# First phase of a hybrid decoder layer: column-group order of two small matmul blocks, GpSimd's elementwise work on other engines, and new places of the side steps

## Chip, cores and metric

The kernel runs on one core of one Trainium2 chip. The metric is the device time of one execution in microseconds (us). Engines are named as in the profile: PE (TensorE), PEld (its weight loads), DVE (VectorE), ACT (ScalarE), POOL (GpSimd), SP (SyncE, which here only issues DMAs).

## What is computed

One layer for 512 tokens of width 1024. The part that the change touches is the first phase: an input projection, two recurrent mixers (HGRN2 and S5) and two gates. In the reference, cut to this part:

```python
h = _rmsnorm(x, norm_mix_g)
q_raw, f_raw, i_raw, og_raw, u_raw, gate_hg, gate_s5 = jnp.split(h @ w_in, SPLITS, axis=-1)
# HGRN2, 4 heads of 128, chunks of 64 tokens
f = lb + (1.0 - lb) * sigmoid(f_raw); k = 1.0 - f; q = silu(q_raw)
b = cumsum(log(f)) within a chunk
scores = (q * exp(b - b_ref)) @ (k * exp(b_ref - b)).T, lower triangle
o = scores @ v + (q * exp(b)) @ S_prev
S  = decay * S_prev + (k * exp(b_last - b)).T @ v
y_hg = o * rsqrt(mean(o * o)) * norm_g * silu(og_raw)
# S5, 32 groups: x_t = Abar x_{t-1} + Bbar u_t,  y_t = Re(C x_t) + D u_t
g = gelu(y); y_s5 = g * sigmoid(g @ glu_w + glu_b)
merged = sigmoid(gate_hg) * (y_hg @ w_branch_hg) + sigmoid(gate_s5) * (y_s5 @ w_branch_s5)
```

Behind it come an output projection, a conv-gated MLP, a per-layer embedding and a last norm. The change does not touch them.

## The kernel before

**Big matmuls.** Every product with a weight matrix is made of three matmuls in fp32r (L231 to L233, the function `mm3`): weights and activations are split into a high and a low part, and high times high, high times low and low times high are added in PSUM. I call such a group of three a triple. Weights come in chunks through SP's DMA queue; ACT makes the high part and DVE the low part of each chunk (`split`, L243 and L244), up to three chunks ahead of their use.

**Order on PE.** PE's instructions are issued in the order in which the program is written (`manual_schedule`). For the other engines the framework's scheduler chooses the order, by its own estimate of times, at most guided by `high_priority`. The main line of the first phase is `phase_u` (32 triples for the S5 input u, then 8 for f of head 0), then the pieces in `ORDER`: projections of heads h0 to h3 (f, q, og, 8 triples each), v (32), and eight gates g0 to g7 (16 each).

**Side steps.** The mixers' small matmuls are woven into the main line by a planner. `clock` counts estimated microseconds: 0.65 for each triple, and 1.7 ns for each stationary or moving column, whichever are more, for each small matmul. After each triple, `tick` looks at the side generators (`hg_all`, `s5_side`, `r1_side`); one whose due time has come runs up to its next `yield`, and the value that it yields is the delay until its next step. The table `WAIT` holds these delays. A head of HGRN2 takes these steps: its elementwise chain (`hg_side`, L487 to L518), `psc` (scores), `pk` (transposes), `pu` (state updates), `pso` (outputs), `pms` (sum of squares). A block of S5 takes: tables Fr, Fi, Hr, Hi (`s5_tables`, L724 to L743), `ps5k` (kernel), `ps5t` (transposes), `ps5v` (inputs to states, then a scan on DVE), `ps5y` (outputs). All small matmuls are in plain fp32; each shows in the trace as two records. L172 is the helper `mm`, so they are told apart by their tiles.

**Column groups.** An output that starts at PSUM partition 0, 32, 64 or 96 and has 64 or 32 stationary columns occupies a part of PE's columns, a column group. `ps5v` (L777) already takes its two 64-column groups in turn, and `ps5k` (L747, L750) its four 32-column groups. `psc` takes for each of four token tiles five matmuls: one of 64 columns between the two chunks, two of 64, two of 32. `ps5y` takes for each of four pairs of groups Fr, two T and Fi, all with 128 stationary columns.

**Elementwise work on GpSimd.** L496, L497, L513, L573 and L574 of each head, L725, L728, L739 and L742 of each S5 block. GpSimd also issues the DMAs of u, of the S5 kernels (`d_k`, then T) and of the S5 outputs.

**Set-up of S5.** `s5_setup` (L616 to L701), some hundred small DVE instructions at high priority, issued behind `phase_u` in the program.

Of the kernel before, what the change touches and what calls it, by code (L numbers as in the profile page):

```python
# [8 lines left out]
F32 = mybir.dt.float32  # L9
F32R = mybir.dt.float32r  # L10
I32 = mybir.dt.int32
AF = mybir.ActivationFunctionType
ALU = mybir.AluOpType
# [3 lines left out]
P = 128  # L17
# [15 lines left out]


WAIT = {
    "r": [16.5, 17.5],
    "hg": [[19.5, 3.5, 4.5, 5, 7],
           [13.5, 3.5, 5.5, 5, 10],
           [18.0, 4, 4, 5.5, 7.5],
           [22.0, 3.5, 4, 9, 6.5]],  # L40
    "s5": [[20, 0, 2, 13, 0],
           [9, 2, 16.5, 12.5, 4.0],
           [7, 1.5, 5.5, 15, 0],
           [5, 4.0, 12.5, 14, 12.0]],
}

ORDER = "h0 v h1 g0 h2 g1 g2 h3 g3 g4 g5 g6 g7".split()
# [66 lines left out]
def hybrid_kernel(ctx: ExitStack, tc: tile.TileContext, a):  # L114
# [56 lines left out]
    def mm(out, w, x, start=True, stop=True, **kw):  # L171
        E.matmul(out, w, x, start=start, stop=stop, **kw)  # L172
        clock[0] += max(w.shape[-1], x.shape[-1]) * 1.7e-3
# [8 lines left out]
    def split_w(i):  # L182
        split_w_.pop(i)()

    early = {}

    def w_chunk(i, off):
        n = chunk_size(plan[i])
# [6 lines left out]
    def emit_w(dst=None):  # L195
        i = wstate["next"]
        n = chunk_size(plan[i])
        off = wstate["off"]
        wst = early.pop(i, None)
        if wst is None:  # L200
            wst = wp.tile([P, CW], F32, tag="wst", bufs=2, name=f"wst{i}")
            nc.sync.dma_start(wst[:, :n], w_chunk(i, off))
        if dst:
            whi, wlo = dst
        else:
            whi = wp.tile([P, CW], F32R, tag="whi", bufs=LOOK + 1, name=f"whi{i}")
            wlo = wp.tile([P, CW], F32R, tag="wlo", bufs=LOOK + 1, name=f"wlo{i}")

        def do():
            split(whi[:, :n], wlo[:, :n], wst[:, :n])  # L210

        if i < 3:
            split_w_[i] = do
        else:
            with tc.high_priority():
                do()
        wstate["off"] += P * n
        wstate["next"] += 1
        return whi, wlo
# [21 lines left out]
    def split(hi, lo, src):  # L241

        S.activation(hi, src, AF.Copy)  # L243
        V.tensor_tensor(out=lo, in0=src, in1=hi.bitcast(F32), op=ALU.subtract)  # L244

    def act_pair(name):
        return (ap_.tile([P, KD, T], F32R, tag="ahi", name=name + "h"),
# [237 lines left out]
    def hg_side(h):  # L485
# [3 lines left out]
        S.activation(sq, q, AF.Sigmoid)  # L489
        so_ = hgt("e1", h)  # L490
        S.activation(so_, og, AF.Sigmoid)
        V.tensor_scalar(out=f, in0=f, scalar1=olb[:, h:h + 1], scalar2=lbt[:, h:h + 1],
                        op0=ALU.mult, op1=ALU.add)
        kk = hgt("kk", h)
        V.tensor_scalar(out=kk, in0=f, scalar1=-1.0, scalar2=1.0, op0=ALU.mult, op1=ALU.add)
        G.tensor_tensor(out=q, in0=q, in1=sq, op=ALU.mult)  # L496
        G.tensor_tensor(out=og, in0=og, in1=so_, op=ALU.mult)  # L497
        S.activation(f, f, AF.Ln)
        b = hgt("b", h)
        V.tensor_tensor_scan(out=b, data0=smask, data1=f, initial=0.0, op0=ALU.mult, op1=ALU.add)  # L500
# [9 lines left out]
        kc = f  # L510
        V.tensor_tensor(out=kc, in0=f, in1=kk, op=ALU.mult)
        V.tensor_tensor(out=e2, in0=e2, in1=kk, op=ALU.mult)
        G.tensor_tensor(out=e1, in0=e1, in1=q, op=ALU.mult)  # L513
        V.tensor_tensor(out=q, in0=q, in1=b, op=ALU.mult)
        qa, ka, qb = e1, e2, q
        dec = ch(b)[:, :, CH - 1]
# [7 lines left out]
        HC = CH // 2  # L524
        for t in range(4):
            c0 = t * P
            mm(psc[0:CH, c0 + CH:c0 + P], kc[:, c0:c0 + CH], qb[:, c0 + CH:c0 + P])
            for n, x0 in ((CH, HC), (HC, 0)):
                for o in (CH, 0):
                    mm(psc[o:o + n, c0 + o + x0:c0 + o + x0 + HC], ka[:, c0 + o:c0 + o + n],  # L530
                       qa[:, c0 + o + x0:c0 + o + x0 + HC])

        V.tensor_tensor(out=pr(kc)[:, :, 0], in0=pr(kc)[:, :, 0],
                        in1=bc(pr(b)[:, :, 1, CH - 1:CH], P, 4, CH), op=ALU.mult)
# [35 lines left out]
        S.activation(osq, pso, AF.Square)  # L570
        osh = hgt("e1", h, dt=F32R)
        osl = hgt("e2", h, dt=F32R)
        G.tensor_scalar(out=osh, in0=osq, scalar1=1.0, scalar2=0.0, op0=ALU.mult, op1=ALU.add)  # L573
        G.tensor_tensor(out=osl, in0=osq, in1=osh.bitcast(F32), op=ALU.subtract)  # L574
        yield WAIT["hg"][h][4]
        pms = small_ps("pms")
        E.matmul(pms, onesr, osh, start=True, stop=False)
# [32 lines left out]
    def tmp2(*shape):  # L610
        n = math.prod(shape)
        names = "abc"[:len(shape)]
        pat = f"p ({' '.join(names)}) -> p {' '.join(names)}"
        return [t[:, :n].rearrange(pat, **dict(zip(names, shape))) for t in tv]

    def s5_setup():  # L616
# [67 lines left out]
        V.tensor_tensor(out=ni, in0=ni, in1=tq, op=ALU.subtract)  # L684
        V.tensor_tensor(out=nr, in0=nr, in1=den, op=ALU.mult)
        V.tensor_tensor(out=ni, in0=ni, in1=den, op=ALU.mult)
        t1, t2 = tmp2(GP, 16)
        cmul(V, br_, bi_, bc(nr.unsqueeze(2), P, GP, 16), bc(ni.unsqueeze(2), P, GP, 16), bcp[:, 0], bcp[:, 1],
             t1, t2)
# [24 lines left out]
    def s5_tables(b):  # L714
        gs = slice(b * 4, b * 4 + 4)
        Fr = sp.tile([P, 4, 9, 16], F32, tag="Fr", name=f"Fr{b}")
        Fi = sp.tile([P, 4, 9, 16], F32, tag="Fi", name=f"Fi{b}")
        sh = (P, 4, 9, 16)
        cr = bc(bcp[:, 2, gs].unsqueeze(2), *sh)
        ci = bc(bcp[:, 3, gs].unsqueeze(2), *sh)  # L720
        ar = bc(Ar[:, gs].unsqueeze(3), *sh)
        ai = bc(Ai[:, gs].unsqueeze(3), *sh)
        t1, t2 = tmp2(4, 9, 16)
        V.tensor_tensor(out=t1, in0=cr, in1=ar, op=ALU.mult)  # L724
        G.tensor_tensor(out=t2, in0=ci, in1=ai, op=ALU.mult)  # L725
        V.tensor_tensor(out=Fr, in0=t1, in1=t2, op=ALU.subtract)
        V.tensor_tensor(out=t1, in0=cr, in1=ai, op=ALU.mult)
        G.tensor_tensor(out=t2, in0=ci, in1=ar, op=ALU.mult)  # L728
        V.scalar_tensor_tensor(out=Fi, in0=t1, scalar=-1.0, in1=t2, op0=ALU.mult, op1=ALU.subtract)
        Hr = sp.tile([P, 4, 8, 16], F32, tag="Hr", name=f"Hr{b}")  # L730
        Hi = sp.tile([P, 4, 8, 16], F32, tag="Hi", name=f"Hi{b}")
        sh = (P, 4, 8, 16)
        ar = bc(Ar[:, gs, 1:9].unsqueeze(3), *sh)
        ai = bc(Ai[:, gs, 1:9].unsqueeze(3), *sh)
        br = bc(br_[:, gs].unsqueeze(2), *sh)
        bi = bc(bi_[:, gs].unsqueeze(2), *sh)
        t1, t2 = tmp2(4, 8, 16)
        V.tensor_tensor(out=t1, in0=ar, in1=br, op=ALU.mult)
        G.tensor_tensor(out=t2, in0=ai, in1=bi, op=ALU.mult)  # L739
        V.tensor_tensor(out=Hr, in0=t1, in1=t2, op=ALU.subtract)  # L740
        V.tensor_tensor(out=t1, in0=ar, in1=bi, op=ALU.mult)
        G.tensor_tensor(out=t2, in0=ai, in1=br, op=ALU.mult)  # L742
        V.tensor_tensor(out=Hi, in0=t1, in1=t2, op=ALU.add)  # L743
        yield WAIT["s5"][b][0]
        pk = small_ps("ps5k")
        for i in range(4):
            E.matmul(pk[i * 32:(i + 1) * 32, 0:P], Bbr[:, b * 4 + i],  # L747
                     Fr[:, i, 1:9].rearrange("p t q -> p (t q)"), start=True, stop=False)
        for i in range(4):
            E.matmul(pk[i * 32:(i + 1) * 32, 0:P], Bbi[:, b * 4 + i],  # L750
                     Fi[:, i, 1:9].rearrange("p t q -> p (t q)"), start=False, stop=True)
        clock[0] += 0.6
        kt = sp.tile([P, 8, 16], F32, tag="kt", name=f"kt{b}")
        S.activation(kt, pk[:, 0:P].rearrange("p (t q) -> p t q", t=8), AF.Copy)
        V.scalar_tensor_tensor(out=kt[:, 7], in0=e16, scalar=d16[:, b:b + 1], in1=kt[:, 7],
                               op0=ALU.mult, op1=ALU.add)
        G.dma_start(d_k[b].rearrange("p g t -> g p t")[:, :, 0:128], kt.rearrange("p t q -> p (t q)"))
        G.dma_start(bigs[b][1], dram_ap(d_k, b * 16 * 8 * 240, [[16, 8], [240, P], [1, P]]))
        yield WAIT["s5"][b][1]
        et = sp.tile([P, 2, 4, P], F32, tag="et", name=f"et{b}")  # L760
        for ri, h_ in enumerate((Hr, Hi)):
            pt = small_ps("ps5t")
            for i in range(4):
                E.transpose(pt[:, i * P:(i + 1) * P], h_[:, i].rearrange("p s q -> p (s q)"), ident)
            S.activation(et[:, ri], pt.rearrange("p (g n) -> p g n", g=4), AF.Copy)
        Fb[b] = (Fr, Fi, et)
        yield WAIT["s5"][b][2]

    def s5_states(b):
# [36 lines left out]
        yield WAIT["s5"][b][3]  # L806
        py = small_ps("ps5y")
        for i in range(4):
            gp = b * 4 + i
            o = py[:, i * P:(i + 1) * P]  # L810
            mm(o, Fr[:, i, 0:8].rearrange("p t q -> p (t q)"), st[:, 0, i].rearrange("p r c -> p (r c)"),
                     start=True, stop=False)
            for r in range(2):
                g = gp * 2 + r
                mm(o[:, r * NC5:(r + 1) * NC5], bigs[b][1][:, i * 2 + r], bigs[b][0][:, i * 2 + r], start=False, stop=False,
                         skip_group_check=True)
            mm(o, Fi[:, i, 0:8].rearrange("p t q -> p (t q)"), st[:, 1, i].rearrange("p r c -> p (r c)"),
                     start=False, stop=True)
        yl = bigs[b][2]
        S.activation(yl, py.rearrange("p (g c) -> p g c", g=8), AF.Copy)  # L820
        G.dma_start(lifted(d_y, b), yl)
# [66 lines left out]
    phase_u()  # L888
    hg_setup()
    with tc.high_priority():  # L890
        s5_setup()
    for b in range(4):
        s5_load(b)
    hg = side(hg_all())
# [310 lines left out]
```

## Time and profile before

| what | value |
|---|---|
| time, median of 3 runs | 791.29 us (791.24 to 791.9) |
| profiled execution, its own time | 792.42 us |
| its span, first to last instruction | 790.3 us |
| PE busy | 772.0 us, 98% of the span |
| DVE, ACT, POOL busy | 520.6, 358.9, 104.8 us |
| mean granted TensorE clock | 0.994 |

The first phase fills about the first 283 us of the span. In a row of groups, the columns are line, engine, operation, tiles (out<-in), shapes and count, then busy us and mean ns of one, then the engine's idle us just before them and what ended it. In the timeline the columns are start us, us, engine, line, operation; rows with a count are merged. Matmuls are pipelined, so their durations overlap, and what one costs is read from start to start.

### The profile page before, as it was taken

How to read it: one execution, taken by the hardware profiler on the slowest of the kernel's cores; microseconds unless marked ns; L12 is line 12 of the kernel's file. 1: busy time of each engine (PE TensorE's matmuls, PEld its weight loads, DVE VectorE, ACT ScalarE, POOL GpSimd, SP SyncE). 2: the span in 40 equal slices, each digit the busy share in tenths (PEclk: the TensorE clock that was granted, in tenths of full speed). 3: DMA queues.
4: the chain of work that ended last, by engine and by line, in shares of the span. 5: the costliest groups of instructions: out<-in, count | busy, mean ns of one | idle time of the engine just before them, and what ended most of it. 6: DMA issues, size and time to landing. Idle time of an engine off the chain costs nothing.

```text
span 790.3 us, 9971 instructions
## 1 busy us (share of the span) xinstructions
PE 772.0 (98%) x3806; PEld 638.4 (81%) x3806; DVE 520.6 (66%) x827; ACT 358.9 (45%) x470; POOL 104.8 (13%) x133
## 2 busy tenths in 40 slices
PE   9899999999999999999999999999999999999996
PEld 7687877888888778888888888888888888888885
DVE  7998885888583576475887667776677134243654
ACT  7345373563753942253543434434444133233565
POOL 2044351331521100032000000000000001010000
PEclk9999999999999999999999999999999999999999
DMA  9472424223343233523232232232332333224511
GB/s 339 161 186 79 131 67 111 81 70 99 102 104 107 74 107 106 193 101 107 80 107 94 93 107 84 103 108 81 107 99 88 93 94 107 69 93 140 178 53 54
DMA packets 27039, 86.10 MB, mean 109 GB/s; under 512 B 4720, under 2 KB 4864, under 8 KB 26992
## 3 DMA queue, kind: packets, MB, share of 16 engines
q1 hardware_dynamic: 22608, 77.58, 29.9%
q0 software_dynamic: 3664, 6.84, 3.9%
q10 hardware_dynamic: 720, 1.05, 0.4%
q8 instruction: 30, 0.49, 0.3%
q14 instruction: 17, 0.14, 0.1%
HBM read 80.72 MB, written 4.69 MB: 108 GB/s over the span
## 4 chain that ended last, share of the span: by engine, by line
PE 71%; DMA 2%; ACT 2%; DVE 1%; issue 1%; POOL 0%; DVEq 0%; ACTq 0%
PE pdn L233 5%; PE pdn L231 5%; PE pdn L232 5%; PE puv L231 5%; PE pug L231 5%; PE puv L233 5%; PE pug L233 5%; PE pug L232 5%; PE puv L232 5%; PE pw L233 2%; PE pw L231 2%; PE pw L232 2%; DMA yT<-d_y 2%; PE pgh L231 1%; PE pga L231 1%
## 5 line engine op out<-in xcount | busy, mean ns | idle before, releaser
L243 ACT ACTIVATE whi<-wst 128x1024 fp32r<-128x1024 f32 (+1 forms) x124 | 129.0, 1040 | 262.7 <-issue 74.6
L244 DVE TENSOR_TENSOR wlo<-wst,whi 128x1024 fp32r<-128x1024 f32 (+1 forms) x124 | 157.7, 1272 | 121.7 <-ACT whi L243 121.7
L231 PE MATMUL pdn<-gh,whi 128*128 128x512 f32 x176 | 69.0, 392 | 0.0
L233 PE MATMUL pdn<-gh,wlo 128*128 128x512 f32 x176 | 68.5, 389 | 0.0
L232 PE MATMUL pdn<-gl,whi 128*128 128x512 f32 x176 | 68.5, 389 | 0.0
L231 PE MATMUL pug<-x1gh,whi 128*128 128x512 f32 x160 | 62.2, 389 | 0.0
L232 PE MATMUL pug<-x1gl,whi 128*128 128x512 f32 x160 | 62.2, 389 | 0.0
L233 PE MATMUL pug<-x1gh,wlo 128*128 128x512 f32 x160 | 62.2, 389 | 0.0
L231 PE MATMUL puv<-x1gh,whi 128*128 128x512 f32 x160 | 62.2, 389 | 0.0
L232 PE MATMUL puv<-x1gl,whi 128*128 128x512 f32 x160 | 62.2, 389 | 0.0
L233 PE MATMUL puv<-x1gh,wlo 128*128 128x512 f32 x160 | 62.2, 389 | 0.0
L947 POOL TENSOR_TENSOR sqs<-sqs,sq 128x512 f32<-128x512 f32 x14 | 23.2, 1658 | 217.7 <-ACT sq L946 217.3
L985 DVE TENSOR_TENSOR u<-pug,R 128x512 f32<-128x512 f32 x20 | 13.8, 692 | 38.3 <-PE pug L233 38.3
L233 PEld LDWEIGHTS pdn<-gh,wlo 128*128 128x128 f32 x176 | 33.0, 188 | 6.9
L232 PEld LDWEIGHTS pdn<-gl,whi 128*128 128x128 f32 x176 | 33.1, 188 | 6.7
L231 PEld LDWEIGHTS pdn<-gh,whi 128*128 128x128 f32 x176 | 33.0, 188 | 6.6
L233 PEld LDWEIGHTS puv<-x1gh,wlo 128*128 128x128 f32 x160 | 30.0, 188 | 6.3
L232 PEld LDWEIGHTS pug<-x1gl,whi 128*128 128x128 f32 x160 | 30.0, 188 | 6.3
L233 PEld LDWEIGHTS pug<-x1gh,wlo 128*128 128x128 f32 x160 | 30.0, 188 | 6.3
L232 PEld LDWEIGHTS puv<-x1gl,whi 128*128 128x128 f32 x160 | 30.0, 188 | 6.3
L231 PEld LDWEIGHTS puv<-x1gh,whi 128*128 128x128 f32 x160 | 30.0, 188 | 6.2
L231 PEld LDWEIGHTS pug<-x1gh,whi 128*128 128x128 f32 x160 | 30.0, 188 | 6.1
(398 smaller groups left out, 1810.8 us busy)
## 6 DMA issues: line engine op xcount, KB each, us to landing
wst<-W SPq DMA_DIRECT2D x126, 512.0 KB, 3.3
xt<-x SPq DMA_DIRECT2D x4, 512.0 KB, 9.0
T<-d_k POOLq DMA_DIRECT2D x4, 512.0 KB, 8.7
xr<-xT SPq DMA_DIRECT2D x4, 512.0 KB, 6.7
wst<-W SPq DMA_DIRECT2D x6, 256.0 KB, 2.7
xs<-xT SPq DMA_DIRECT2D x4, 256.0 KB, 4.8
xs<-xT SPq DMA_DIRECT2D x2, 512.0 KB, 6.7
d_u<-uT POOLq DMA_DIRECT2D x4, 256.0 KB, 4.5
```

Source lines behind the costliest of these rows:

```text
L231: E.matmul(out, wh, xh, start=start, stop=False)
L232: E.matmul(out, wh, xl, start=False, stop=False)
L233: E.matmul(out, wl, xh, start=False, stop=stop)
L243: S.activation(hi, src, AF.Copy)
L244: V.tensor_tensor(out=lo, in0=src, in1=hi.bitcast(F32), op=ALU.subtract)
L947: G.tensor_tensor(out=sqs, in0=sqs, in1=sq, op=ALU.add)
L985: V.tensor_tensor(out=u[:, 2:], in0=ps[i], in1=Rt, op=ALU.mult)
```

## The change

The table of delays gets new values. The set-up of S5 is cut in two, and DVE's share of the second half (from L687 on) is queued behind the low part of weight chunk 6, the first chunk of head 0. In the scores, each 32-column group gets a matmul of its own. In `ps5y` each matmul with 128 stationary columns becomes two with 64, in turn. GpSimd's elementwise instructions go to DVE, one of them (the rounding of the squares) to ACT; the affine step of f goes from DVE to ACT.

```diff
 WAIT = {
-    "r": [16.5, 17.5],
-    "hg": [[19.5, 3.5, 4.5, 5, 7],
-           [13.5, 3.5, 5.5, 5, 10],
-           [18.0, 4, 4, 5.5, 7.5],
-           [22.0, 3.5, 4, 9, 6.5]],
-    "s5": [[20, 0, 2, 13, 0],
-           [9, 2, 16.5, 12.5, 4.0],
+    "r": [16.5, 11.5],
+    "hg": [[19.5, 3.5, 7, 5, 8.5],
+           [13.5, 3.5, 5.5, 9, 10],
+           [18, 4, 5, 5.5, 7],
+           [21.5, 7.5, 5.5, 9, 8]],
+    "s5": [[21.5, 0, 2, 13, 0],
+           [9, 2, 16.5, 12.5, 2.5],
            [7, 1.5, 5.5, 15, 0],
-           [5, 4.0, 12.5, 14, 12.0]],
+           [5, 0, 12.5, 14, 12]],
 }
...
         def do():
-            split(whi[:, :n], wlo[:, :n], wst[:, :n])
+            lo_ins[i] = split(whi[:, :n], wlo[:, :n], wst[:, :n]).ins
...
-        V.tensor_scalar(out=f, in0=f, scalar1=olb[:, h:h + 1], scalar2=lbt[:, h:h + 1],
-                        op0=ALU.mult, op1=ALU.add)
+        S.activation(f, f, AF.Identity, scale=olb[:, h:h + 1], bias=lbt[:, h:h + 1])
...
-        G.tensor_tensor(out=q, in0=q, in1=sq, op=ALU.mult)
-        G.tensor_tensor(out=og, in0=og, in1=so_, op=ALU.mult)
+        V.tensor_tensor(out=q, in0=q, in1=sq, op=ALU.mult)
+        V.tensor_tensor(out=og, in0=og, in1=so_, op=ALU.mult)
...
-        G.tensor_tensor(out=e1, in0=e1, in1=q, op=ALU.mult)
+        V.tensor_tensor(out=e1, in0=e1, in1=q, op=ALU.mult)
...
         for t in range(4):
             c0 = t * P
+            for o in range(0, P, HC):
+                cc = slice(c0 + o, c0 + o // CH * CH + CH)
+                mm(psc[o:o + HC, cc], ka[:, c0 + o:c0 + o + HC], qa[:, cc])
             mm(psc[0:CH, c0 + CH:c0 + P], kc[:, c0:c0 + CH], qb[:, c0 + CH:c0 + P])
-            for n, x0 in ((CH, HC), (HC, 0)):
-                for o in (CH, 0):
-                    mm(psc[o:o + n, c0 + o + x0:c0 + o + x0 + HC], ka[:, c0 + o:c0 + o + n],
-                       qa[:, c0 + o + x0:c0 + o + x0 + HC])
...
-        G.tensor_scalar(out=osh, in0=osq, scalar1=1.0, scalar2=0.0, op0=ALU.mult, op1=ALU.add)
-        G.tensor_tensor(out=osl, in0=osq, in1=osh.bitcast(F32), op=ALU.subtract)
+        split(osh, osl, osq)
...
+        def rest():
+            with tc.issue_after(lo_ins[6]):
+                s5_setup2(nr, ni, cs, sn)
+        return rest
+
+    def s5_setup2(nr, ni, cs, sn):
         t1, t2 = tmp2(GP, 16)
...
-        G.tensor_tensor(out=t2, in0=ci, in1=ai, op=ALU.mult)
+        V.tensor_tensor(out=t2, in0=ci, in1=ai, op=ALU.mult)
...
             o = py[:, i * P:(i + 1) * P]
-            mm(o, Fr[:, i, 0:8].rearrange("p t q -> p (t q)"), st[:, 0, i].rearrange("p r c -> p (r c)"),
-                     start=True, stop=False)
-            for r in range(2):
-                g = gp * 2 + r
-                mm(o[:, r * NC5:(r + 1) * NC5], bigs[b][1][:, i * 2 + r], bigs[b][0][:, i * 2 + r], start=False, stop=False,
-                         skip_group_check=True)
-            mm(o, Fi[:, i, 0:8].rearrange("p t q -> p (t q)"), st[:, 1, i].rearrange("p r c -> p (r c)"),
-                     start=False, stop=True)
+
+            hs = [(slice(q * 64, (q + 1) * 64), slice(q * 4, (q + 1) * 4)) for q in range(2)]
+            for ri, F in ((0, Fr), (2, None), (1, Fi)):
+                for q, tq in hs:
+                    if F is not None:
+                        mm(o[q], F[:, i, tq].rearrange("p t q -> p (t q)"), st[:, ri, i].rearrange("p r c -> p (r c)"),
+                           start=ri == 0, stop=ri == 1, skip_group_check=True)
+                if F is None:
+                    for r in range(2):
+                        g = i * 2 + r
+                        for q, tq in hs:
+                            mm(o[q, r * NC5:(r + 1) * NC5], bigs[b][1][:, g, q], bigs[b][0][:, g],
+                               start=False, stop=False, skip_group_check=True)
...
-        s5_setup()
+        s5_setup()()
```

Of the four table products that move from GpSimd to DVE in each S5 block, one is shown; the others (L728, L739, L742) are changed in the same way.

More of the change, by code (lines that the diff above doesn't have):

```diff
@@ L183, in split_w @@
         split_w_.pop(i)()
-    early = {}
+    early, lo_ins = {}, {}
     def w_chunk(i, off):
@@ L243, in split @@
         S.activation(hi, src, AF.Copy)
-        V.tensor_tensor(out=lo, in0=src, in1=hi.bitcast(F32), op=ALU.subtract)
+        return V.tensor_tensor(out=lo, in0=src, in1=hi.bitcast(F32), op=ALU.subtract)
     def act_pair(name):
@@ L724, in s5_tables @@
         V.tensor_tensor(out=t1, in0=cr, in1=ar, op=ALU.mult)
-        G.tensor_tensor(out=t2, in0=ci, in1=ai, op=ALU.mult)
+        V.tensor_tensor(out=t2, in0=ci, in1=ai, op=ALU.mult)
         V.tensor_tensor(out=Fr, in0=t1, in1=t2, op=ALU.subtract)
         V.tensor_tensor(out=t1, in0=cr, in1=ai, op=ALU.mult)
-        G.tensor_tensor(out=t2, in0=ci, in1=ar, op=ALU.mult)
+        V.tensor_tensor(out=t2, in0=ci, in1=ar, op=ALU.mult)
         V.scalar_tensor_tensor(out=Fi, in0=t1, scalar=-1.0, in1=t2, op0=ALU.mult, op1=ALU.subtract)
@@ L738, in s5_tables @@
         V.tensor_tensor(out=t1, in0=ar, in1=br, op=ALU.mult)
-        G.tensor_tensor(out=t2, in0=ai, in1=bi, op=ALU.mult)
+        V.tensor_tensor(out=t2, in0=ai, in1=bi, op=ALU.mult)
         V.tensor_tensor(out=Hr, in0=t1, in1=t2, op=ALU.subtract)
         V.tensor_tensor(out=t1, in0=ar, in1=bi, op=ALU.mult)
-        G.tensor_tensor(out=t2, in0=ai, in1=br, op=ALU.mult)
+        V.tensor_tensor(out=t2, in0=ai, in1=br, op=ALU.mult)
         V.tensor_tensor(out=Hi, in0=t1, in1=t2, op=ALU.add)
@@ L808, in s5_states @@
         for i in range(4):
-            gp = b * 4 + i
             o = py[:, i * P:(i + 1) * P]
-            mm(o, Fr[:, i, 0:8].rearrange("p t q -> p (t q)"), st[:, 0, i].rearrange("p r c -> p (r c)"),
-                     start=True, stop=False)
-            for r in range(2):
-                g = gp * 2 + r
-                mm(o[:, r * NC5:(r + 1) * NC5], bigs[b][1][:, i * 2 + r], bigs[b][0][:, i * 2 + r], start=False, stop=False,
-                         skip_group_check=True)
-            mm(o, Fi[:, i, 0:8].rearrange("p t q -> p (t q)"), st[:, 1, i].rearrange("p r c -> p (r c)"),
-                     start=False, stop=True)
+            hs = [(slice(q * 64, (q + 1) * 64), slice(q * 4, (q + 1) * 4)) for q in range(2)]
[10 more added lines that the diff above has]
+                               start=False, stop=False, skip_group_check=True)
         yl = bigs[b][2]
```

## The prediction

> **What bounds the kernel.** I read the page first, then PE's waits, then windows for the clock, then the timeline at each wait and at each small block.
>
> ```profile
> span 790.3 us, 9971 instructions
> PE 772.0 (98%) x3806; PEld 638.4 (81%) x3806; DVE 520.6 (66%) x827; ACT 358.9 (45%) x470; POOL 104.8 (13%) x133
> ```
>
> PE is busy in 98% of the span. So time comes out of this kernel in two ways only: less work on PE, or less of the 18 us in which PE stands. The list of PE's waits (total us, times, longest) names what ends those:
>
> ```profile
> PE pf L233 <- DVE wlo L244: 3.4, 1, 3.4
> PE pbs L231 <- ACT s5oh L243: 1.7, 1, 1.7
> PE psc L172 <- DVE q L514: 1.4, 1, 1.4
> PE pms L578 <- POOL e L574: 1.2, 1, 1.2
> ...
> PE pk L547 <- DVE f L533: 1.0, 1, 1.0
> PE pms L577 <- POOL e L573: 0.7, 1, 0.7
> PE psc L172 <- DVE d L518: 0.4, 1, 0.4
> ```
>
> All lie in the first phase. Two cost more than they show, by the windows (length, PE busy and count, granted clock, DMA):
>
> ```profile
> 30.00:36.00 6.00, 4.29 (x12) 0.73 0.48 152
> 50.00:60.00 10.00, 10.00 (x45) 1.00 0.90 203
> 120.00:124.40 4.40, 4.40 (x33) 0.67 0.44 134
> 260.70:262.70 2.00, 0.83 (x2) 1.00 0.33 119
> ```
>
> A full window issues a big matmul each 0.222 us, so a triple takes 0.67. Behind the 3.4 us wait the clock is 0.73 for 6 us, which costs 0.27 x 6 = 1.6; behind the waits of psc (1.8 together) it is 0.67 for 4.4 us, 0.33 x 4.4 = 1.5. The waits of pms, 1.9 together, show no drop. So the first wait is worth 5.0, psc's 3.3.
>
> **PE's own work.** In the timeline of PE, a part of one quarter of a ps5y block, then ps5k and ps5v, then the end of a psc block:
>
> ```profile
> 196.68 0.56 PE L172 MATMUL ps5y<-uy,T 128*128 128x64 f32 x4
> 197.08 0.44 PE L172 MATMUL ps5y<-st,Fi 128*128 128x128 f32 x2
> ...
> 206.75 0.43 PE L747 MATMUL ps5k<-Fr,Bbr 128*32 128x128 f32 x8
> 206.99 0.40 PE L750 MATMUL ps5k<-Fi,Bbi 128*32 128x128 f32 x8
> ...
> 226.86 1.15 PE L172 MATMUL ps5v<-uy,et 128*64 128x64 f32 x32
> ...
> 230.94 0.26 PE L172 MATMUL psc<-e,e 128*32 128x32 f32 x4
> 231.13 0.27 PE L172 MATMUL psc<-q,f 128*64 128x64 f32 x1
> 231.66 0.50 PE L231 MATMUL pgh<-xgh,whi 128*128 128x512 f32 x1
> ```
>
> ps5y: eight records of 128 stationary columns. T starts at 196.68, four records later Fi at 197.08: 0.10 to 0.11 each, although T moves 64 columns and Fr and Fi 128. So a quarter costs 8 x 0.11 = 0.89 us, a block 3.6. After the change a quarter has 16 records of 64 columns, in turn. T's eight go by ps5v, which has their exact form: 1.15 / 32 = 0.036, so 0.29. Fr and Fi (eight, moving 128) have no row of their own; ps5k moves 128 as well, and its first eight records, two rounds over its four groups, take from 206.75 to 206.99, 0.12 a round. A pair on two groups is one round: four rounds of 0.11 to 0.12, 0.46 together. Quarter 0.75, saving 0.14; 16 quarters 2.2. The other end: if Fr's halves run one behind the other, eight records at 0.11 make 0.88, the quarter 1.17, and the change loses 4.5.
>
> [...]
>
> psc: a token tile now costs 0.53 (231.13 to 231.66 is 64-column part, 32-column part and the pause at each change of width; the 32-column part alone is 230.94 to 231.13, 0.19). After it, eight 32-column records with their four groups (0.19 to 0.25, since they move up to 64) and two of 64 columns, with the same two pauses. The two go by what the 64-column part now takes with six records, 0.53 - 0.19 = 0.34, as its upper end, and 0.2 as its lower. So 0.39 to 0.59 for 0.53: I take 0.50, saving 0.03 x 16 = 0.5, with ends of -2.2 and +1.0.
>
> **The first wait.** The mixed timeline around it:
>
> ```profile
> 24.92 1.06 ACT L243 ACTIVATE whi<-wst 128x1024 fp32r<-128x1024 f32 x1
> 25.49 0.42 DVE L592 TENSOR_TENSOR tv<-nr,s5p 128x256 f32<-128x256 f32 x1
> 30.43 1.23 DVE L244 TENSOR_TENSOR wlo<-wst,whi 128x1024 fp32r<-128x1024 f32 x1
> 31.71 0.50 PE L233 MATMUL pf<-xgh,wlo 128*128 128x512 f32 x1 [3.44 <-DVE wlo L244]
> ```
>
> The high part of chunk 6 is there at 25.98, but DVE is in the second half of S5's set-up, which begins at 25.49, and makes the low part only at 30.43. The change puts exactly this half behind that low part, which then is ready at 25.98 + 1.23 = 27.2; PE wants it at 31.71 - 3.44 = 28.27. The wait goes, with its slow clock: 5.0 us. The new wait holds DVE from 25.49 to 25.98 at most; behind it stand only the set-up and what the scheduler finds meanwhile. The value 11.5 of "r" moves nothing: the step is due at 16.9 + 11.5 = 28.4 by the planner's clock, and `finish` runs it at 40 x 0.65 = 26.0, as before.
>
> What is late next? DVE, on the way to the first psc and ps5t:
>
> ```profile
> 58.26 5.50 DVE L244 TENSOR_TENSOR wlo<-wst,whi 128x1024 fp32r<-128x1024 f32 x1
> ...
> 67.42 2.31 DVE L244 TENSOR_TENSOR wlo<-wst,whi 128x1024 fp32r<-128x1024 f32 x1
> ...
> 75.65 0.69 DVE L743 TENSOR_TENSOR Hi<-tv,tv 128x512 f32<-128x512 f32 x1 [0.96 <-POOL tv L742]
> ```
>
> Hi is used by ps5t as soon as it is there, so it has nothing to spare, and PE now comes 5.0 earlier. DVE loses the excess of the two low parts over 1.23 (4.3 + 1.1), this wait on GpSimd and one at Hr (1.5 together) and the affine step (0.7); it gets seven products of 0.69 (three of the head, four of the tables), 4.8. Net 2.8 less up to Hi, and ps5t0 comes one triple later (0.7). So 5.0 - 2.8 - 0.7 leaves a new wait of 1.5; the scheduler can fill some of DVE's idle time in the start, so I take 1.0, with ends of 0 and 3.4 (what was removed).
>
> **GpSimd's work on DVE.** The groups of the first 290 us:
>
> ```profile
> L244 DVE TENSOR_TENSOR wlo<-wst,whi 128x1024 fp32r<-128x1024 f32 (+1 forms) x42 | 59.4, 1415 | 9.9 <-ACT whi L243 9.9
> L738 DVE TENSOR_TENSOR tv<-Ar,bbr 128x512 f32<-128x512 f32 x4 | 6.5, 1612 | 0.1
> L743 DVE TENSOR_TENSOR Hi<-tv,tv 128x512 f32<-128x512 f32 x4 | 4.9, 1228 | 3.2 <-POOL tv L742 3.2
> L740 DVE TENSOR_TENSOR Hr<-tv,tv 128x512 f32<-128x512 f32 x4 | 2.8, 692 | 2.1 <-POOL tv L739 1.9
> L729 DVE SCALAR_TENSOR_TENSOR Fi<-tv,tv 128x576 f32<-128x576 f32 x4 | 3.0, 755 | 3.2 <-POOL tv L728 3.2
> L574 POOL TENSOR_TENSOR e<-kk,e 128x512 fp32r<-128x512 f32 x4 | 6.0, 1510 | 0.3
> ```
>
> Added: per block two products at 0.755 and two at 0.69, four blocks 11.6; per head four at 0.69, 11.0; less the four affine steps, which I set at 0.69 as well, 2.8. Together 19.8 us. Removed: the excess of low parts over the 1.23 of the quoted one (42 x 0.185 = 7.8), of L738 and L743 over L740's 0.69 (3.7 and 2.1), and 8.3 us of DVE's waits on GpSimd (3.2 + 3.2 + 1.9): 21.9. So DVE's load stays, while each chain gets shorter, since a product of GpSimd takes 1.5 us (L574) and one of DVE 0.69. ACT gets eight passes of about 0.6 (half of the 1.06 above), 5 us in 280 at 45%: nothing, covered by its idle time. GpSimd keeps only DMA issues and small fills; its d_k and T issues no longer stand behind products.
>
> **Places.** By the planner's clock, with triples counted from the start: psc1 moves from behind triple 133 to 136, while DVE's table work for block 1 starts at 111 as before: 2.0 us more room. Its wait was 1.8 and the chain does not grow, so it goes, with its clock: -3.3 (ends 0 and -3.3). psc2 stays at 196 and its head starts two triples later (171), 1.3 us less room; the chain loses two GpSimd products (-1.6): no wait, at worst 1. pk2 gets seven triples behind psc2 in place of four and ps5v: 4.7 for 3.8 us: the wait of 1.0 falls to 0.2. ps5t3 comes ten triples behind ps5y2 in place of sixteen; the tables of block 3 need 12 products, 8.5 us, against 6.7 plus pso, ps5k and the copies, about 9: I take a new wait of 0.4, ends 0 and 2. pms3 moves behind the last gate, two triples behind pso3 in place of ten; square, copy and subtraction take about 0.6 + 0.6 + 0.7 (half of ACT's 1.06 twice, and L740) and PE has 1.3 to do: a wait of 1.0 for 1.9, ends 0 and 1.9. ps5y3 comes eight triples earlier, which only helps the gelu chain. The other moves shift pk, pu, pso and ps5v, which nothing in the list of waits names beyond pk2, by up to ten triples: nothing. The wait of pbs (1.7) sits behind ACT's queue in the tail; I leave it, ends -1.7 and +1.4.
>
> **Sum**, on the profiled execution (792.42): -2.2 - 0.5 (PE's work) - 5.0 + 1.0 (start) - 3.3 (psc1) - 0.8 (pk2) + 0.4 (ps5t3) - 0.9 (pms3) = -11.3, so 781.1. The median of the runs stands 1.13 lower, at 791.29: 780.0.
>
> **Rivals.** (1) DVE takes the gain of the start back: chance 0.15. Removing a wait helps only where what comes next is ready, and Hi had nothing to spare. New waits at psc0 and ps5t0 of 3.4 with a slow clock of 1.6 instead of 1.0: 784.0. For it: that Hi is already waited for; against it: the two long low parts, which get shorter. (2) The halves run one after the other: 4.5 lost for 2.2 gained, 786.7, chance 0.05; ps5v's 0.036 speaks against it. (3) A ps5y block halves: 4 x 3.57 / 2 = 7.1 saved for 2.2, 775.1, chance 0.04. [...] (4) Each record has a floor, so that twice as many cost more; the dearest per record among the narrow blocks is psc, ten in 0.53: 64 x 0.053 = 3.4 a block, 0.7 saved for 2.2, 781.5, chance 0.03. [...] (5) The other side: DVE's long instructions are not due to GpSimd's products but to its DMA issues, which stay. Then 19.8 us come onto DVE and 8.3 go. Per chain that ends in a psc, about 4.8 more against 2 less: at psc0 and ps5t0 a wait of 5.0 + 2.8 with clock 1.6, at psc1 1.8 + 2.8 - 2.0 with 1.5, at psc2 2.8 + 1.3 with 1.5. Those are 9.4 + 4.1 + 5.6 = 19.1 for the 1.0 of the sum, so 798. It turns slower where about two thirds of the excess stay (11.3 of 18.1). Against it: L738 and L740 have one form, L738 starts together with a product of GpSimd (L739) and takes 1.61, L740 has waited for that product and takes 0.69. Chance 0.07. (6) Nothing moves, since the scheduler orders DVE so that each old wait comes back under another name: 791 less PE's 2.7, at 788 to 791, chance 0.06.
>
> **Numbers.** The forecast has 0.60: 780.0. The low end takes rival 3 or all stalls gone, 775; the high end rivals 1, 2 and 4, 787. Rivals 5 and 6 lie outside. About 0.2%, 1.6 us, is what a measurement of this kernel can tell from none. Faster 0.88, same 0.05 (most of it from 6), slower 0.07.
>
> **What would show it.** Right: no wait of pf on wlo, clock 1.00 from 30 to 36 and from 120 to 125; ps5y blocks near 3.0 us; low parts at 1.22 throughout; L738 and L743 at 0.69; waits, if any, at psc0, ps5t0, ps5t3, pms3. Wrong: ps5y at 3.6 or more, psc above 2.2 a block, long low parts beside GpSimd's DMA issues, a slow clock behind a new wait.

## The result, and the profile after

| | before | after |
|---|---|---|
| median of the runs on that chip | 791.6 us | 783.87 us (three runs, 783.49 to 784.47) |
| profiled execution, its own time | 792.42 us | 783.87 us |
| its span | 790.3 us | 782.1 us |
| mean granted clock | 0.994 | 0.995 |

The ratio of the times is 0.9901, with a 95% interval of 0.9881 to 0.992: 7.8 us less. A fourth execution of the changed kernel took 959.49 us at a granted clock of 0.753 and is left out; with it the median is 784.17, from which the expectations below start. The forecast was 780.0 us; its sum asked for -11.3 us, and the span of the profiled execution lost 8.2.

The page of after, the two lines that answer to those of before:

```profile
span 782.1 us, 10200 instructions
PE 767.3 (98%) x3934; PEld 631.8 (81%) x3934; DVE 519.5 (66%) x855; ACT 371.6 (48%) x483; POOL 55.2 (7%) x97
```

PE is busy 4.7 us less, although it issues 128 records more: 3.1 of it is shorter blocks, most of the rest less time at a slow clock (1.7 us lost to it, for 1.6 + 1.5 in before). DVE does what it did before (519.5 for 520.6) while GpSimd's work halves. PE's waits in after (total us, times, longest):

```profile
PE ps5t L768 <- DVE Hi L747: 2.7, 1, 2.7
PE pms L574 <- ACT e L243: 1.6, 1, 1.6
...
PE pms L575 <- DVE e L244: 0.9, 1, 0.9
PE pbs L232 <- DVE s5ol L244: 0.6, 1, 0.6
PE pbs L231 <- ACT s5oh L243: 0.4, 1, 0.4
...
PE pf L233 <- DVE wlo L244: 0.2, 1, 0.2
```

The 3.4 us of pf (but for 0.2), the 1.8 of psc and the 1.0 of pk are gone, and pbs waits 1.0 in place of 1.9. A wait of 2.7 at ps5t0 is new (0.3 before), and the two of pms have grown from 1.9 to 2.5. Windows of after (length, PE busy and count, PEld, DVE, ACT and POOL likewise, granted clock, DMA share, GB/s):

```profile
30.00:36.00 6.00, 6.00 (x32) 5.09 (x31) 5.25 (x19) 2.13 (x2) 0.00 (x0) 1.00 0.57 182
70.00:80.00 10.00, 7.28 (x77) 5.44 (x76) 7.36 (x17) 2.04 (x5) 1.31 (x2) 1.00 0.21 65
120.00:124.40 4.40, 4.40 (x22) 3.63 (x21) 0.90 (x4) 1.90 (x4) 0.00 (x0) 1.00 0.87 176
250.00:260.00 10.00, 7.46 (x27) 5.58 (x27) 4.76 (x6) 9.88 (x11) 0.00 (x0) 0.83 0.31 105
```

Both slow stretches of before are at 1.00 now. A new one lies behind pms3: 0.83 in 10 us is 1.7 us lost on top of the waits.

PE's rows of one quarter of a ps5y block and the start of the next, and of two token tiles of psc, in the timeline of after:

```profile
67.53 0.31 PE L172 MATMUL psc<-e,e 128*32 128x64 f32 x8
...
68.03 0.31 PE L172 MATMUL psc<-e,e 128*32 128x64 f32 x8
...
185.35 0.44 PE L172 MATMUL ps5y<-st,Fr 128*64 128x128 f32 x4
185.62 0.40 PE L172 MATMUL ps5y<-uy,T 128*64 128x64 f32 x8
185.85 0.39 PE L172 MATMUL ps5y<-st,Fi 128*64 128x128 f32 x4
186.07 0.39 PE L172 MATMUL ps5y<-st,Fr 128*64 128x128 f32 x4
```

A quarter takes 186.07 - 185.35 = 0.72 (0.75 forecast), a block 2.83 from its first start to the start of the next big matmul, for 3.49 before. A token tile takes 68.03 - 67.53 = 0.50, exactly as forecast.

### The profile page after: what moved, and what is told of

The parts are those of the page before. It is cut to its first block, busy times and chain, and to the rows that moved or that the text cites. A ratio compares the mean times of both kernels' runs of the same rounds, so it can differ in the third digit from the quotient of the medians.

```text
span 782.1 us, 10200 instructions
## 1 busy us (share of the span) xinstructions
PE 767.3 (98%) x3934; PEld 631.8 (81%) x3934; DVE 519.5 (66%) x855; ACT 371.6 (48%) x483; POOL 55.2 (7%) x97
## 4 chain that ended last, share of the span: by engine, by line
PE 85%; DVE 6%; DMA 4%; ACT 2%; issue 2%; SPq 0%; POOL 0%; ACTq 0%; DVEq 0%
PE pdn L231 5%; PE pdn L232 5%; PE pdn L233 5%; PE puv L232 5%; PE pug L232 5%; PE puv L231 5%; PE pug L231 5%; PE pug L233 5%; PE puv L233 5%; PE pw L233 2%; PE pw L232 2%; PE pw L231 2%; DVE wlo L244 2%; PE pgs L231 2%; PE pgh L231 2%
## 5 line engine op out<-in xcount | busy, mean ns | idle before, releaser
L244 DVE TENSOR_TENSOR wlo<-wst,whi 128x1024 fp32r<-128x1024 f32 (+1 forms) x124 | 148.4, 1197 | 127.3 <-ACT whi L243 127.2
```

Source lines behind the costliest of these rows:

```text
L244: return V.tensor_tensor(out=lo, in0=src, in1=hi.bitcast(F32), op=ALU.subtract)
```

## The experiments

### The four parts alone

The change falls into four parts that together are the whole of it. Each was put into the kernel before by itself (before: 791.85 us on that chip). Each ratio below is to before on the chip of that run, with its 95% interval of 0.7 to 1.5 us to either side; what is smaller between two runs isn't told apart.

**The cut of the S5 set-up alone.**

```diff
-        s5_setup()
+        s5_setup()()
```
(and `s5_setup` split at L687 as in the change).

> The kernel before with one part of the change alone: the second half of S5's set-up queued behind the low part of weight chunk 6. Theory A (DVE's chain decides what the removed wait is worth): the wait of pf on wlo (3.4 us) and its slow clock go, 4.9 us as in the profile after; but GpSimd's products still lengthen DVE's chain, so psc0 and ps5t0 wait 3 to 5 us more, and the whole is 0 to 2 us faster than before (789 to 791). Theory B (the parts are independent and add up): 4.9 us faster, 786.5, with ps5t0 waiting 2.5 as after or less.

Measured: 794.68 us, ratio 1.0038 (1.0026 to 1.0049). PE's waits in this run, and a window with its clock:

```profile
PE ps5t L771 <- DVE Hr L747: 2.0, 1, 2.0
...
PE ps5t L771 <- DVE Hi L750: 1.2, 1, 1.2
...
PE ps5k L757 <- DVE Fi L736: 1.0, 1, 1.0
```

```profile
70.00:80.00 10.00, 5.74 (x54) 4.08 (x51) 7.93 (x12) 3.37 (x6) 4.64 (x3) 0.77 0.17 62
```

The wait of pf is gone, but PE stands at ps5k and ps5t instead (4.2 us with a clock of 0.77). Theory A had these waits, but not the clock: all of PE's waits in the first 300 us are 8.3 us, less than the 10.2 of before, and the profiled execution is longer since PE has half its clock for 17.1 us of them, for 6.8 in before (the last section says how that comes in steps). So alone the cut makes the kernel slower.

**The column groups alone** (the matmuls of psc and ps5y as in the change).

```diff
+            hs = [(slice(q * 64, (q + 1) * 64), slice(q * 4, (q + 1) * 4)) for q in range(2)]
+            for ri, F in ((0, Fr), (2, None), (1, Fi)):
+                for q, tq in hs:
...
```

> The kernel before with the new psc and ps5y matmuls alone. Both theories: ps5y blocks 2.83 us for 3.49, psc 2.00 for 2.13, 3.2 us of work less. Theory A: psc1, which waits for DVE, waits about 0.7 us longer, since the ps5y in front of it got shorter, and the total is 2 to 3 us less (788.3 to 789.3). Theory B: all 3.2 us arrive, 788.1.

Measured: 790.27 us, ratio 0.9983 (0.9975 to 0.9992), 1.3 of the 3.1 us that PE has less to do (4 x 0.66 and 4 x 0.13), less than either theory. The wait of psc grew, from 1.8, and 2.6 us of waiting at psg are new, while those at pms, pk and pbs are gone:

```profile
PE psc L172 <- DVE d L518: 3.3, 1, 3.3
```

**GpSimd's elementwise work alone** (to DVE and ACT).

```diff
-        G.tensor_tensor(out=e1, in0=e1, in1=q, op=ALU.mult)
+        V.tensor_tensor(out=e1, in0=e1, in1=q, op=ALU.mult)
```

> The kernel before with GpSimd's elementwise work on DVE and ACT alone. Theory A (DVE's long instructions come from GpSimd's products): low parts at 1.23 us and the table products at 0.69 throughout; the waits of psc1 (1.8, with 1.5 of slow clock) and pk2 (1.0) go or shrink, pms3 (1.9) shrinks, the wait of pf (3.4) stays: 3 to 5 us faster, 786 to 788. Rival from the prediction (the long instructions come from DMA issues, DVE gets 20 us more): slower than before, over 793.

Measured: 789.29 us, ratio 0.9963 (0.995 to 0.9977). So the work did not make DVE the limit, and rival 5 falls. Theory A's 3 to 5 us were a little high: pk2's wait and a part of pms3's went (1.3 left), but psc1 still waits 1.6 us, with a slow clock behind it (0.97 from 120 to 160).

**The table of delays alone.**

> The kernel before with the new table of delays alone. Theory A: psc1 gets 2.0 us more room and loses its wait and slow clock (-3.3); pms3, two triples behind pso3 in place of ten, waits longer, 3 to 5 us with GpSimd's 2.1 us of rounding and difference, perhaps with a slow clock: total between -1 and +3 us, 790 to 794. Theory B (each new place removes a wait): 787 to 788.

Measured: 802.88 us, ratio 1.0143 (1.013 to 1.0156), the largest effect of the four and a loss. Its longest wait:

```profile
PE psc L172 <- DVE d L518: 5.9, 1, 5.9
```

Both theories fail. The 5.9 us are at psc1, the place for which the prediction had counted 2.0 us more room. What it had not counted is that the new places change DVE's order too. Head 1's scan (L500), on the way to psc1, begins at 111.78 in before; here two gate steps (L878), for the first of which DVE stands 1.9 us, and two low parts come in front of it:

```profile
115.43 1.22 DVE L500 TENSOR_TENSOR_SCAN b<-ph,f 128x512 f32<-128x512 f32 x1
```

Alone the four parts come to +3.0 - 1.3 - 2.9 + 11.3 = about +10 us (from the ratios); together they give -7.8. Costing each part by itself and adding up cannot give the result.

### Column groups, GpSimd and the start in company

The other way round: one part taken out of, or changed in, the kernel after (783.87 us).

**The two halves of ps5y one after the other.** Each column group takes its eight records, then the other group its eight.

```diff
-            for ri, F in ((0, Fr), (2, None), (1, Fi)):
-                for q, tq in hs:
+            for q, tq in hs:
+                for ri, F in ((0, Fr), (2, None), (1, Fi)):
```

> The changed kernel, but ps5y takes all eight records of the first column group, then all eight of the second, in place of in turn. If the saving comes from two groups working at the same time only when they are issued in turn: each record of 64 columns stands alone, T about 0.058 us, Fr and Fi about 0.11, a quarter 1.36 for 0.71, a block 5.4 us for 2.83, the kernel about 10 us slower than after (794). If PE overlaps groups whatever the order, or if the halves are cheap by themselves: a block stays near 2.8 and the time at 784.

Measured: 783.35 us (0.9898, 0.9879 to 0.9917), a block 3.54 us. Taking the groups in turn is worth 0.7 us a block, and without it the block is as long as before, not longer as was expected. PE's timeline shows why:

```profile
93.86 0.28 PE L172 MATMUL ps5y<-st,Fi 128*64 128x128 f32 x1
93.91 0.27 PE L172 MATMUL ps5y<-st,Fr 128*64 128x128 f32 x1
93.97 0.27 PE L172 MATMUL ps5y<-st,Fi 128*64 128x128 f32 x1
```

Fr of the next half starts between the two records of Fi of the half before, so the halves overlap at the seam. The 2.8 us lost on four blocks don't show in the time: the waits of pms3 fell to 0.2 with no slow clock behind them (0.998 over the span, 0.995 in after), ps5t0's to 1.8. The latter is chance: in this execution the clock rose to 1.00 at 9.5 us for 5.7, so PE came 1.1 us later to what follows.

**GpSimd's work back** on GpSimd, the rest of the change kept.

> The changed kernel with GpSimd's elementwise products, rounding and the affine step back where they were. Theory A (DVE's chains, shortened by this part, are what lets the other parts pay): low parts and table products get long again (5 us and 1.6 us), psc0, ps5t0, psc1 and pms3 wait 2 to 6 us each, 798 to 806, at the level of the new places alone (802.9) or above. Theory B (parts add up): 2.9 us slower than after, 787.

Measured: 795.6 us (1.0057, 1.0044 to 1.0071), some 12 us above after, where the same edit alone was worth 2.9: below theory A's 798 to 806, far above theory B's 787. The longest waits (the first at psc1, the second at ps5t0), and a group of the first 290 us on DVE:

```profile
PE psc L172 <- DVE d L518: 3.2, 1, 3.2
PE ps5t L770 <- DVE Hr L746: 2.0, 1, 2.0
```

```profile
L744 DVE TENSOR_TENSOR tv<-Ar,bbr 128x512 f32<-128x512 f32 x4 | 6.3, 1569 | 0.1
```

In after the low parts of the same stretch and that group read

```profile
L244 DVE TENSOR_TENSOR wlo<-wst,whi 128x1024 fp32r<-128x1024 f32 (+1 forms) x43 | 51.4, 1194 | 15.6 <-ACT whi L243 15.5
```

```profile
L742 DVE TENSOR_TENSOR tv<-Ar,bbr x4: 684/692/694, 69.7 to 191.0; 128x512 f32<-128x512 f32 x4
```

So DVE's long instructions come from GpSimd's products: 1.57 us beside one, 0.69 without, with GpSimd's DMA issues in both kernels. The low parts take 1317 ns on average with GpSimd's work back, 1194 without. What of a product of GpSimd holds DVE up, no run shows.

**The start uncut**, the rest of the change kept.

```diff
-        s5_setup()()
+        s5_setup()
```

> The changed kernel without the cut of the S5 set-up: all of the set-up stands ahead of the low part of chunk 6 again. Theory A (the start's gain of 4.9 is real but pays for the wait at ps5t0): the wait of pf with its slow clock comes back (+4.9), the wait of 2.7 at ps5t0 goes, since PE comes 4.9 later to it (-2.4): 786.7, between 785.5 and 788. Theory B (the cut moves DVE's load, and the rest of the change needs it): ps5t0 still waits, 789 or more. Theory C (the start's gain is wholly taken back): 784 to 785.

Measured: 783.41 us (0.9903, 0.9888 to 0.9918). The wait of pf is back (3.1 us), and the time is the same as with the cut: nearest to theory C. DVE up to the Hi of block 0, and PE's use of it, without the cut:

```profile
71.35 0.68 DVE L739 TENSOR_TENSOR tv<-Ai,bbr 128x512 f32<-128x512 f32 x1
72.06 0.69 DVE L740 TENSOR_TENSOR Hi<-tv,tv 128x512 f32<-128x512 f32 x1
...
76.81 0.60 PE L761 MATMUL ps5t<-sm,Hi 128*128 128x128 f32 x4
```

and in after:

```profile
72.31 1.22 DVE L244 TENSOR_TENSOR wlo<-wst,whi 128x1024 fp32r<-128x1024 f32 x1
...
74.05 0.42 DVE L531 TENSOR_TENSOR f<-f,b 128x256 f32<-128x256 f32 x1
74.39 0.68 DVE L747 TENSOR_TENSOR Hi<-tv,tv 128x512 f32<-128x512 f32 x1
...
75.12 0.66 PE L768 MATMUL ps5t<-sm,Hi 128*128 128x128 f32 x4 [2.72 <-DVE Hi L747]
```

Without the cut Hi is ready at 72.75, 4.06 us before PE wants it. With it PE wants it at 75.12 - 2.72 = 72.40, 4.4 earlier, and Hi is ready at 75.07, 2.3 later: 4.4 + 2.3 - 4.06 = 2.7, the wait. Up to Hi DVE does one low part more with the cut (1.2 us) and a half of the pk chain (f, 0.42); the other 0.7 of the 2.3 isn't assigned. The likely reason, which no run took apart, is that a PE that is earlier also asks for its next weights earlier; DVE has hardly a gap to spare (busy 19.76 of the 20 us from 40 to 60 in after). By the starts of the same big matmuls, the 4.5 us gained at pf are given back as 2.9 at ps5t0 and 1.9 at pms3, where this run waits 2.2 us with no slow clock behind (1.00 from 250 to 260).

**The old table of delays**, the rest of the change kept.

> The changed kernel with the old table of delays; everything else of the change stays. Theory A (the new places and the shorter chains belong together: alone the places cost 11.0 us, in company they pay): psc1 is due at triple 133 again, three triples earlier, with the chain no shorter than before, so its wait of about 1.8 with 1.5 of slow clock comes back (+3.3); ps5t0 comes 1.5 us earlier and waits about 1.0 more; pk2's wait comes back (+0.8); pms3, ten triples behind pso3 again, loses its 2.5 and the slow clock of 1.7 (-3 to -4). Sum 784.2 + 5.1 - 3.5 = 786, between 784 and 789. Theory B (the other parts carry the gain and the places give nothing): no wait at psc1, since GpSimd's products are gone; 784.2 - 3.5 = 780 to 781.

Measured: 791.74 us (1.001, 1.0 to 1.0021). Its three longest waits:

```profile
PE psg L231 <- ACT gh L243: 5.9, 1, 5.9
PE ps5t L768 <- DVE Hi L747: 2.7, 1, 2.7
PE psc L172 <- DVE e L511: 2.1, 1, 2.1
```

The places are worth 7.9 us in company, where alone they cost 11; theory A had a loss of 2 (786), B a gain. psc1's wait is back as theory A had it (2.1, and a clock of 0.72 from 118 to 124). ps5t0 waits 2.7 as in after, but here with a slow clock behind it (0.71 from 74 to 84). The larger loss was in neither theory, at psg: by this table ps5y3 begins at 240.44 in place of 228.34, and the chain of copies, DMAs and gelus behind it delivers its last gh late:

```profile
265.16 0.61 ACT L243 ACTIVATE gh<-gf 128x512 fp32r<-128x512 f32 x1
```

PE stands for it until 265.83; in after that gh is begun at 251.63. The prediction said of this move that it "only helps the gelu chain", and gave it no price. In before, with the same place, PE begins psg at 264.06, here at 257.71, so the chain is now what is late.

### What still waits

**ps5t0 three triples later,** behind pk0, which keeps its place.

```diff
-    "s5": [[21.5, 0, 2, 13, 0],
+    "s5": [[21.5, 2.5, 2, 10.5, 0],
```

> The changed kernel with ps5t0 and pk0 in exchanged places: ps5t0 three triples later, behind pk0, ps5v0 four triples later, the rest as it was. If the wait of ps5t0 (2.7 us) is DVE's chain to Hi, the place moves by 2.0 + 0.4 us and the wait shrinks to 0 to 0.8: 1.5 to 2.5 us faster than after, unless pk0 now waits for the same DVE (then it moves there: less than 1 us). If the wait comes from PE's place in DVE's order alone, it follows ps5t0 and nothing is gained.

Measured: 779.95 us (0.9853, 0.9839 to 0.9868), 3.9 below after. The wait is gone; nothing takes its place. It is more than the 1.5 to 2.5 expected: by the starts of the same big matmuls 3.0 come at ps5t0, where Hi is ready just in time, and 0.9 at pms3, whose first wait shrinks from 1.6 to 0.7.

**pms3 later, behind the start of the S5 output gate** (`finish(hg)` behind `s5_glu()`, the last delay of head 3 at 3 instead of 8).

> The changed kernel with pms3 inside the GLU's matmuls: its delay is 3 in place of 8 and the last finish of the head's side comes behind s5_glu. If the 2.5 us wait of pms3 and the slow clock behind it (1.7 us by the windows) are due to its place two triples behind pso3: both go, 3 to 4 us faster than after at best; the norm of head 3 comes 3 us later and must still meet the first branch matmul 10 us on. Rival: the wait moves to the branch matmuls or to the GLU's own outputs, since ACT is the one that is late, and at most 1 us is left.

Measured: 782.05 us (0.988, 0.9866 to 0.9895), 1.8 below after. The waits of pms and the slow clock behind them go (2.5 and 1.7 us), and so do the 1.0 of pbs, but pbh, which needs the norm that pms3 feeds, now waits 1.4 and 0.8 with a slow clock behind: the rival, though 1.8 us are left where it had at most 1. ps5t0's wait is 2.1 for 2.7, but here a slow clock follows it (over the span the clock is 0.993, for 0.995 in after).

**Both** (the expectation says "earlier" of pms3, which is later in the program, as in the run before, and moves pk0, which stays; its 4.2 and 2.1 start from 784.17).

> The changed kernel with pk0 and ps5t0 three triples later and with pms3 earlier in the program, behind the S5 outputs' gate (the two edits that gave 4.2 and 2.1 us alone). Theory A (far apart in time, they add): 784.2 - 6.3 = 778. Theory B (they interact by the scheduler's order on DVE and ACT, as the four parts of the change do): the wait at pbh grows or another appears, 780 to 783.

Measured: 779.13 us (0.9844, 0.983 to 0.9858): between the two theories, and not told apart from the first edit alone (0.8 us less). The waits at pbh are as in the run before (1.4 and 0.8), and the clock is 0.83 from 260 to 270, behind them.

**Head 3's state updates and outputs earlier**, with ps5t0 later.

```diff
-           [21.5, 7.5, 5.5, 9, 8]],
+           [21.5, 7.5, 3, 6, 8]],
```

> The changed kernel with pk0 and ps5t0 three triples later (as in the run that gave 779.95) and with head 3's state updates and outputs some seven triples earlier, so that pms3 stands about nine triples behind pso3 and at its own place in the program. Theory A (pms3's waits and the slow clock behind them are a matter of its distance to pso3, since the square stands in ACT's queue behind a gelu and a weight's high part): the waits of 0.9 and 0.7 go, and the slow clock of about 1.5 with them; nothing later waits, since the norm comes earlier too: 779.95 - 3.1 = 777, between 776 and 778. Theory B (ACT's queue in the last 20 us before the S5 gate is the limit, whichever instruction is late): the waits come back at psg on gh or at pso, 780 or more.

Measured: 779.16 us (0.985, 0.9835 to 0.9865), not told apart from ps5t0 later alone. The waits did not go:

```profile
PE pms L574 <- ACT e L243: 0.9, 1, 0.9
PE pms L575 <- DVE e L244: 0.8, 1, 0.8
```

In this run pso3 ends 5.8 us earlier than in the run with only ps5t0 later (its last matmul starts at 241.23 for 247.00), but ACT comes to its square at 246.63, five us behind, and to the square's high part at 248.64, for 248.18 and 248.80 in that run. Theory A is wrong: not the distance to pso3 decides, but ACT's queue, which holds the gelus, the high parts and a gate's sigmoid in front. So theory B had the cause; its place for the waits (psg, pso) was wrong, and its 780 a little high. The slow clock did go in the profiled execution (1.00 from 250 to 260, for 0.83 with only ps5t0 later), though the waits behind which it had stood are the same.

## Why the prediction was right, and where it was wrong

The sign and the range were right; the point was 4 us too low. By its own terms, in us of the profiled execution (the measured ones from the waits, the windows, the blocks' lengths and the starts of big matmuls; the first row from the first matmul of pq, 39.29 before and 34.69 after, with 0.25 for the later begin of the run):

| step | forecast | measured |
|---|---|---|
| first wait and its clock | -5.0 | -4.85 |
| new wait at ps5t0 | +1.0 | +2.4 (2.7 for 0.3) |
| ps5y | -2.2 | -2.6 (4 x 0.66) |
| psc | -0.5 | -0.5 (4 x 0.13) |
| psc1's wait and clock | -3.3 | -3.7 |
| pk2 | -0.8 | -1.0 |
| ps5t3 | +0.4 | 0 |
| pms3 | -0.9 | +2.3 (waits +0.6, clock +1.7) |
| pbs | 0 | -0.9 |
| sum | -11.3 | -8.9; the span says -8.2 |

Of the 0.7 between the last two, 0.3 is the later begin of the first big matmul; the rest isn't assigned. Two terms are far off, ps5t0 by +1.4 and pms3 by +3.2, and smaller ones make up for half of that.

**PE's own work: right,** term by term. Fr and Fi take 0.44 to 0.49 a quarter (0.46 forecast), T 0.23 where 0.29 was taken from ps5v. The halving of a block in rival 3, from which the low end of 775 was taken, no run shows: 3.49 to 2.83 is 1.23x, and Fr and Fi, which move 128 columns, fill 0.49 of a quarter's 0.72. The floor of 0.053 a record in rival 4 is not seen either: 2.83 us for 64 records is 0.044 each. The end that was feared, halves one behind the other, was mis-sized: such a block takes 3.54, not 4.7, since the halves overlap at each seam.

**DVE instead of GpSimd: right,** in the load (519.5 for 520.6), the low parts (1194 ns on average for 1415) and the table products (0.69 for 1.61). Rival 5 is refuted by the kernel with GpSimd's work alone and by the one with it back.

**The first wait: right in size, wrong in worth.** Its 5.0 hold for before as profiled, where a slow clock of 1.6 followed; with GpSimd's work alone moved pf waits 3.6 us and none follows. The step that failed is "what is late next": the prediction took the chain up to Hi as 2.8 us shorter and the cut as free for DVE. The chain alone did better (Hi at 72.75 without the cut, 76.34 before, 3.6 less). But the cut itself puts Hi 2.3 us later, with another low part and a step of the pk chain ahead of it. "The scheduler can fill some of DVE's idle time in the start" had no row behind it; DVE was busy 19.93 of the 20 us from 40 to 60 in before, 19.76 in after. This is rival 1's mechanism at about half of its price, and no slow clock with it. As the kernel stands the cut is worth nothing; with ps5t0 three triples later 3.9 us come out (no run has that without the cut).

**pms3: the size was wrong.** Its three operations were costed by themselves, 1.0 of wait. In after they stand in queues:

```profile
249.69 1.18 ACT L841 ACTIVATE gf<-yT 128x512 f32<-128x512 f32 x1
250.65 1.07 ACT L243 ACTIVATE whi<-wst 128x1024 fp32r<-128x1024 f32 x1
251.63 0.61 ACT L243 ACTIVATE gh<-gf 128x512 fp32r<-128x512 f32 x1
252.14 0.58 ACT L568 ACTIVATE kk<-pso 128x512 f32<-128x512 f32 x1
252.75 0.63 ACT L243 ACTIVATE e<-kk 128x512 fp32r<-128x512 f32 x1
...
254.83 0.78 PE L575 MATMUL pms<-e,onesr 128*128 128x512 f32 x1 [0.90 <-DVE e L244]
```

The last matmul of pso3 starts at 250.04; ACT works off a gelu, a high part and gh before the square at 252.14. Ten triples had left room for such queues in before, and the prediction didn't name them: it set ACT down as "nothing, covered by its idle time" by its 45% over the span, where ACT is busy 9.88 of the 10 us from 250 to 260. Moving pms3 back moved the wait to pbh, moving pso3 ahead left it where it was.

**Places: right result, half a reason.** psc1's wait went, but not for the two microseconds of room: with the new places alone it is 5.9, with GpSimd's work back 3.2, with GpSimd's work gone and the old places 1.6. It takes both: with both it is gone. And "the other moves: nothing" was true only of after as it is: with the old table, ps5y3's place shows as a wait of 5.9 at psg.

**The sum.** It was built as if its terms were independent. The single parts (+3.0, -1.3, -2.9, +11.3) show that they are not. That it came within 4 us of the time is in part luck: errors of both signs stand in it, and whether a slow clock follows a wait, 1.7 us for each slow step, was not to be foreseen from its length.

## What to carry to other kernels

In a kernel whose order is woven by hand, a wait that is removed only moves PE earlier: before counting it as gained, look at the next hand-over of the engine that had fed PE, with the order that an earlier PE will give that engine. Places and work belong together, and a part tried alone, either way, tells little of its worth in company. Where one late hand-over is left, moving its consumer a few triples back is the cheapest trial: here it gave 3.9 us, for 779.95, faster than both kernels.

## What the runs showed beside

The length of a wait did not tell whether a slow clock follows, and the prediction had priced the clock by the wait that it stood behind. The clock records of the 14 traces say more. In each of them every change of the clock falls a whole number of 3.41 us after the first one, to 0.01 us, and that first one lies anywhere from 4.1 to 10.5 us behind the begin. So in these traces time is cut into steps of 3.41 us that PE's waits do not shift, and within a step the clock is 1.00 or 0.50: a slow step costs a busy PE 0.50 x 3.41 = 1.7 us. The same wait at ps5t0 in the kernel with the old table and in after, by these steps (length, PE busy and so on as above):

```profile
69.47:72.88 3.41, 1.62 (x11) 0.90 (x7) 3.34 (x6) 0.87 (x2) 0.00 (x0) 1.00 0.02 5
72.88:76.29 3.41, 2.45 (x8) 2.16 (x9) 2.37 (x8) 0.60 (x1) 0.60 (x1) 0.50 0.50 154
```

```profile
70.56:73.97 3.41, 1.84 (x23) 1.16 (x18) 3.34 (x5) 0.88 (x2) 0.00 (x0) 1.00 0.02 5
73.97:77.39 3.42, 2.27 (x12) 1.96 (x13) 2.57 (x9) 0.60 (x1) 0.51 (x1) 1.00 0.48 153
```

With the old table 1.79 of the 2.7 us lie in one step, and the next two are slow; in after 1.57 and 1.15 lie in two, and none is. The same at pms3, with ps5t0 later (waits 0.7 and 0.9, both in one step) and with head 3's steps earlier as well (0.9 and 0.8, with the border between them):

```profile
248.58:251.99 3.41, 1.79 (x7) 1.12 (x7) 3.41 (x6) 3.35 (x5) 0.00 (x0) 1.00 0.48 154
251.99:255.40 3.41, 3.41 (x10) 2.64 (x9) 0.56 (x1) 3.36 (x4) 0.00 (x0) 0.50 0.47 154
```

```profile
246.43:249.84 3.41, 2.50 (x10) 1.50 (x8) 1.77 (x2) 3.41 (x6) 0.00 (x0) 1.00 0.00 0
249.84:253.25 3.41, 2.60 (x11) 2.17 (x12) 3.08 (x5) 3.36 (x4) 0.00 (x0) 1.00 0.40 154
```

Over all 14 traces, from 15 to 300 us, 25 steps at full clock are followed by a slow one. All 13 steps in which PE stands 2.06 us or more are among them, 8 of the 16 with 1.4 to 1.9, and only 4 with less, each of which holds a psc block. What decides between 1.4 and 1.9 us, and why psc blocks count so, stays open; no run moved the moment of a wait and nothing else.

By waits and slow steps the single parts read so (profiled executions, 15 to 300 us):

| kernel | span, us | PE's waits, us | slow steps |
|---|---|---|---|
| before | 790.3 | 10.2 | 2 |
| cut alone | 794.0 | 8.3 | 5 |
| column groups alone | 788.1 | 9.6 | 3 |
| GpSimd's work alone | 788.3 | 8.4 | 2 |
| delays alone | 801.5 | 15.6 | 7 |
| after | 782.1 | 6.5 | 1 |
| ps5t0 later, head 3 earlier | 776.3 | 2.7 | 0 |

Span less waits and 1.7 us a step is 776.5 to 777.2 with the old ps5y and psc blocks and 773.4 to 773.9 with the new ones, so the 3.1 us of the column groups are there in each of them, in company or alone; with the delays alone it is 774.0, which would fit a PE that stands through a part of its slow steps; no run shows that apart. A step more or less is partly the luck of where a wait falls: a difference of 2 us between two profiled executions need not be more than that.
